# Block 1's opening written out in program order, with w_mod cut into four column stages

## The chip, the cores and the metric

The kernel runs on one core of one Trainium2 chip. The metric is the device time of one execution in microseconds (us). Three timed runs of the kernel before gave 1498.35, 1503.71 and 1503.02 us, a median of 1503.02 us. A profiled execution beside them took 1506.47 us.

Five engines work side by side, each through its own list of instructions: TensorE (PE in the profile, PEld for its weight loads), VectorE (DVE), ScalarE (ACT), GpSimd (POOL) and SyncE (SP). SP and POOL start the DMAs here.

## The reference

Two transformer blocks run one after the other on 256 tokens of 1024 channels. The change touches only the start of the first block and one vector used later in it:

```python
silu_c = jax.nn.silu(c); silu_cc = jax.nn.silu(c_ctx)
mod = silu_c @ w_mod[layer] + b_mod[layer]            # 1024 x 6144
sh1, sc1, g1, sh2, sc2, g2 = jnp.split(mod, N_MOD, axis=-1)
mc = jnp.split(silu_cc @ w_mod[layer] + b_mod[layer], N_MOD)
h  = modulate(rms_norm(x,  norm1_w[layer]), sh1, sc1)     # h*(1+scale)+shift
hc = modulate(rms_norm(xc, norm1_w[layer]), mc[0], mc[1])
q, k, v, g, f = split_proj(h @ wi)
kc = hc @ wi[:, K_OFF:V_OFF]; vc = hc @ wi[:, V_OFF:G_OFF]
```

Shift and scale (sh1, sc1) are needed for both sequences before the first projection. The other four parts of mod are needed for c alone, and later: g1 at the end of the mixer, sh2 and sc2 before the FFN, g2 at its end.

## The kernel before

Activations lie transposed, channels on the 128 partitions: a 1024x256 tensor is eight tiles of 128x256 (KT = 8). For full precision every float32 operand is split into a high float32r part (a cast on ACT, line 245) and a low rest (a subtraction on DVE, line 246), and a product is three float32r matmuls. `weights` loads 512 KB of a weight matrix (two k-tiles of 512 columns) into one of four buffers `wf`, by SP, and splits it into one of three pairs `wh`, `wl`. `lin_units` is a generator: each step loads one such piece and issues its matmuls, with the weights stationary (`mm_b`, result transposed, `psb`) or the activations stationary (`mm_a`, result `psa`). A 512-column projection takes four units.

The opening computes shift and scale for both sequences. `mod_first(j)` takes 512 columns of w_mod in four pieces, multiplies them into `psm` with the two conditioning vectors stationary (lines 446 and 447), copies the 4x512 result to SBUF (`mrow`), turns it into columns with four small transposes (`pst`) and adds the bias. Column groups 0 and 1 are the shift, 2 and 3 the scale. Groups 0 and 2 serve the first four k-tiles, 1 and 3 the last four. `normed` then makes the normalized, scaled and shifted tile of each k (`nt` on DVE, `hxh` on ACT, `hxl` on DVE). The string START (line 30) says in which order these steps, the units of the projections q (w_in piece 0, transposed) and f (piece 6), the load of the context and its sums of squares are issued. From this order a scheduler derives the order on each engine.

After the opening comes the projection `win[1]` (k, for both sequences), then `win[2]` and `win[3]` (v), then the eight retention heads, the gates and so on. Beside their units, `mod_rest` computes the other four parts of mod: it loads w_mod in 512 KB pieces through the same four `wf` buffers, accumulates 128x512 products on DVE into `macc` (lines 476 and 478), and sums over the partitions with four matmuls against a column of ones for each 512 columns (line 482), eight times.

The second block and its experts follow. Their instructions stand in the same order in both kernels.

Of the kernel before, what the change touches and what calls it, by code (L numbers as in the profile page):

```python
# [26 lines left out]
NUP = 11  # L27
TOPK = 16
PH = 8
START = "ssssmqmmmnnnnqffhssssxqlfcqfqf"  # L30
GATES = 8
HEADS = (27, 28, 30, 32)
RING = 8
# [115 lines left out]
def _chunks(w, width=512):  # L149

    k, n = w.shape
    return np.ascontiguousarray(w.reshape(k // P, P, n // width, width).transpose(2, 1, 0, 3))


def _layout(i):

    i = {k: np.asarray(v) for k, v in i.items()}
# [9 lines left out]
    a = {  # L167
        "xt": ft(i["x"][0]), "ct": ft(i["ctx"][0]),
        "vec1": v1, "con1": k1, "cv2": v2, "io": io, "dft": _DFT,
        "lora": np.ascontiguousarray(np.concatenate(  # L170
            [np.concatenate([i["rw_w_up_2"][0], i["rw_a_up_2"][0]], axis=0), i["rw_g_up_2"][0]], axis=1)),
        "wmod": _chunks(i["w_mod"][0]), "win": _chunks(i["w_in"][0]),
        "wro": _chunks(i["w_ret_out"][0]), "wfo": _chunks(i["w_four_out"][0]),
        "wbg": _chunks(i["w_branch_gate"][0]), "wo": _chunks(i["w_out"][0]),
        "wup": _chunks(wup),
# [44 lines left out]
class _Builder:  # L220
# [196 lines left out]
    def block1(self, xt):  # L417
        nc, tc, a, S = self.nc, self.tc, self.a, self.S
        V = self.V1
# [7 lines left out]
        mod = cp.tile([P, 48], F32, name="mod")  # L427
        modc = cp.tile([P, 16], F32, name="modc")

        def mod_load(j, k0):  # L430
            wf = self.wp.tile([P, 1024], F32, tag="wf", name="wf", bufs=4).rearrange("p (k n) -> p k n", k=2)
            nc.sync.dma_start(wf, a["wmod"][j][:, k0:k0 + 2])
            return wf

        cs2 = cp.tile([P, KT, 4], F32R, name="cs2")
        self.split(cs, cs2[:, :, :2], cs2[:, :, 2:])

        def mod_first(j):

            ps = self.ps("psm")  # L440
            for k0 in range(0, KT, 2):
                wh, wl = self.weights(a["wmod"][j][:, k0:k0 + 2])
                for k in range(2):

                    s, e = k0 + k == 0, k0 + k == KT - 1
                    nc.tensor.matmul(ps[:4], cs2[:, k0 + k], wh[:, k], start=s, stop=e, skip_group_check=True)
                    nc.tensor.matmul(ps[:2], cs2[:, k0 + k, :2], wl[:, k], start=False, stop=e, skip_group_check=True)
                if k0 + 2 < KT:
                    yield
# [5 lines left out]
            js = slice(4 * j, 4 * j + 4)  # L455
            t = self.tmp([P, 4, 2], "mt")
            nc.vector.tensor_add(t, pt[:, :4, :2], V("bmod")[:, js, None].to_broadcast([P, 4, 2]))
            nc.vector.tensor_add(mod[:, js], t[:, :, 0], pt[:, :4, 2])
            nc.vector.tensor_add(modc[:, js], t[:, :, 1], pt[:, :4, 3])
            yield  # L460

        def mod_rest():

            accs = [S([P, 512], "macc%d" % i) for i in range(2)]
            wf = mod_load(4, 0)
            for j in range(4, 12):
                acc = accs[j % 2]
                for k0 in range(0, KT, 2):
                    w = wf
                    if k0 + 2 < KT:  # L470
                        wf = mod_load(j, k0 + 2)
                    elif j < 11:
                        wf = mod_load(j + 1, 0)
                    for k in range(2):
                        if k0 + k == 0:
                            nc.vector.tensor_scalar(acc, w[:, k], cs[:, 0, 0:1], None, op0=ALU.mult)
                        else:
                            nc.vector.scalar_tensor_tensor(acc, w[:, k], cs[:, k0 + k, 0:1], acc, op0=ALU.mult, op1=ALU.add)  # L478
                    yield
                pt = self.ps("pst")  # L480
                for n in range(4):
                    nc.tensor.matmul(pt[:, n:n + 1], acc[:, n * P:(n + 1) * P], ones[:, 0:1], start=True, stop=True)
                nc.vector.tensor_add(mod[:, 4 * j:4 * j + 4], pt[:, :4], V("bmod")[:, 4 * j:4 * j + 4])
            S.free("macc0", "macc1")
            yield

        rest = mod_rest()

        m1 = cp.tile([P, 2, KT], F32, name="m1")

        def scales(j):
            js = slice(4 * j, 4 * j + 4)
            for i, m in enumerate((mod, modc)):
                nc.vector.scalar_tensor_tensor(m1[:, i, js], m[:, 8 + 4 * j:12 + 4 * j], 1.0, V("n1w")[:, js], op0=ALU.add, op1=ALU.mult)
        first = mod_first(0)
        next(first)
# [18 lines left out]
        nc.scalar.activation(self.warm, f2[:, :1], AF.Sqrt)
        pulls(first, 3)()
        nc.sync.dma_start(xt, a["xt"])
        r = self.rstd(xt)
        first = mod_first(2)
        pulls(first, 4)()  # L520
        scales(0)
        hc = tuple(S([P, KT, T], "hc" + i, F32R) for i in "hl")
# [8 lines left out]
        def fcopy(ps, b):  # L531
            nc.scalar.copy(f[:, b], ps)
        gq = self.lin_units(a["win"][0], KT, 512, bs=[(hx, self.rope(qt, 0.125))])
        gf = self.lin_units(a["win"][6], KT, 512, as_=[(hx, fcopy)])
        second = mod_first(1), mod_first(3)
        work = {"s": soon, "m": second[0], "n": second[1], "q": gq, "f": gf}
        for i in START:
            if i == "x":
                nc.sync.dma_start(xct, a["ct"])
            elif i == "c":  # L540
                self.busy = True
                rc = self.rstd(xct)
                self.busy = False
            elif i == "h":
                scales(1)
            elif i == "l":
                self.C1 = C = self.blob(a["con1"], self.v1c[1], "con1", "blob", self.wid)
            else:
                next(work[i], None)
# [1070 lines left out]
```

## Time and profile before

| what | value |
|---|---|
| profiled execution | 1506.47 us |
| its span | 1504.7 us |
| median of the timed runs | 1503.02 us |
| PE busy in the span | 1352.3 us (90%) |
| DVE busy | 1048.2 us (70%) |
| ACT busy | 739.0 us (49%) |
| granted TensorE clock, mean | 0.975 |
| HBM read | 410.66 MB |

Busy shares are a mean over stages that have different limits. For this change the first 75 us, and then the stretch up to about 310 us in which mod_rest runs, are what is to be read. "PEclk" is the granted clock as a share of the full 2.4 GHz: 0.50 is the lower level of 1.2 GHz. A matmul's listed duration reaches past the start of the next one; what it costs in a row of matmuls is the distance between their starts.

### The profile page before, as it was taken

What the parts mean: (1) busy time and instruction counts of PE and PEld (TensorE: products, weight loads), DVE (VectorE), ACT (ScalarE), POOL (GpSimd) and SP (SyncE); (2) the same over time, 40 slices, a digit from 0 to 9 for tenths busy, and PEclk for the clock granted to TensorE, in tenths of its full rate; (3) what the DMA queues carried; (4) which work ended last, traced back from release to release, by engine and by line L of the source; (5) the groups of instructions that cost most, each with busy time, mean ns of one, the idle gap of its engine ahead of it and who ended that gap; (6) DMA issues with size and microseconds to landing.
All of it is one profiled execution on the core that took longest, in us unless ns stands there. A gap on an engine that the chain in (4) does not pass through costs nothing.

```text
span 1504.7 us, 21103 instructions
## 1 busy us (share of the span) xinstructions
PE 1352.3 (90%) x7496; PEld 975.6 (65%) x7496; DVE 1048.2 (70%) x2095; ACT 739.0 (49%) x1566; POOL 301.3 (20%) x283
## 2 busy tenths in 40 slices
PE   6999999989999999999999789878978898778786
PEld 3788898989999988899889435323533353223222
DVE  6784876867766778656478777778676775767544
ACT  7533554455555676534465355344434353434433
POOL 0000000000000000000000345443444344434341
PEclk9999999999999999999999899999999999999999
DMA  8655575745555453312147699999999999999995
GB/s 289 226 169 181 176 249 192 245 139 183 183 185 187 147 164 118 113 57 90 52 162 251 269 422 420 422 421 421 409 422 420 421 416 420 421 421 421 421 421 237
DMA packets 76569, 413.07 MB, mean 275 GB/s; under 512 B 8641, under 2 KB 8769, under 8 KB 43313
## 3 DMA queue, kind: packets, MB, share of 16 engines
q0 software_dynamic: 38880, 276.59, 44.5%
q1 hardware_dynamic: 37440, 134.88, 27.6%
q8 instruction: 59, 0.97, 0.3%
q14 instruction: 46, 0.37, 0.1%
q10 hardware_dynamic: 144, 0.26, 0.0%
HBM read 410.66 MB, written 1.05 MB: 274 GB/s over the span
## 4 chain that ended last, share of the span: by engine, by line
PE 51%; DMA 19%; DVE 11%; issue 9%; POOL 5%; ACT 4%; POOLq 0%; SPq 0%; DVEq 0%; ACTq 0%
DMA uv<-in_uv_dram,rows 17%; PE psb L267 9%; PE psb L268 9%; PE psb L269 9%; POOL uv L1487 5%; DVE uv L1494 4%; PE acc L1500 3%; DMA wf<-in_wmod_dram 2%; PE psa L277 2%; PE psa L279 2%; PE psa L278 2%; PE acc L267 1%; PE acc L269 1%; PE acc L268 1%; PE psr L1042 1%
## 5 line engine op out<-in xcount | busy, mean ns | idle before, releaser
L1500 PE MATMUL acc<-uv,dg 128*128 128x512 f32 x1024 | 501.9, 630 | 116.8 <-ACT dg L1498 114.2
L1500 PEld LDWEIGHTS acc<-uv,dg 128*128 128x128 f32 x1024 | 188.1, 196 | 419.7 <-ACT dg L1498 251.3
L1494 DVE CUSTOM_DVE_ANT_0 uv<-uv,hn 128x1024 f32<-128x1024 f32 x256 | 310.2, 1222 | 171.7 <-DMA uv<-in_uv_dram,rows 165.7
L1487 POOL DMA_INDIRECT uv<-in_uv_dram,rows x256 | 283.1, 1106 | 395.1 <-PE acc L1500 268.7
L246 DVE TENSOR_TENSOR wl<-wf,wh 128x1024 fp32r<-128x1024 f32 x213 | 258.2, 1217 | 125.8 <-ACT wh L245 122.6
L245 ACT CAST wh<-wf 128x1024 fp32r<-128x1024 f32 x213 | 221.9, 1044 | 237.3 <-PE psb L268 137.4
L267 PE MATMUL psb<-hxh,wh 128*128 128x256 f32 x960 | 280.3, 292 | 4.7 <-ACT hxh L370 3.4
L268 PE MATMUL psb<-hxl,wh 128*128 128x256 f32 x960 | 274.9, 287 | 0.0
L269 PE MATMUL psb<-hxh,wl 128*128 128x256 f32 x960 | 274.1, 286 | 0.2 <-DVE wl L246 0.2
L1495 ACT ACTIVATE act<-act 128x1 f32<-128x1 f32 x256 | 51.8, 202 | 341.4 <-DVE act L1494 341.3
L267 PEld LDWEIGHTS psb<-hxh,wh 128*128 128x128 f32 x960 | 185.4, 193 | 11.2 <-issue 4.7
L268 PEld LDWEIGHTS psb<-hxl,wh 128*128 128x128 f32 x960 | 185.3, 193 | 3.8 <-issue 2.9
L269 PEld LDWEIGHTS psb<-hxh,wl 128*128 128x128 f32 x960 | 185.2, 193 | 1.1 <-issue 0.3
L1498 ACT ACTIVATE dg<-io,act 128x128 f32<-128x128 f32 x256 | 102.8, 402 | 8.4
L1496 ACT ACTIVATE act<-act,gate 128x1 f32<-128x1 f32 x256 | 75.3, 294 | 8.3
L980 POOL MEMSET mt<- 128x2048 f32 x2 | 3.6, 1816 | 351.9 <-PE psb L269 351.9
L478 DVE SCALAR_TENSOR_TENSOR macc<-wf,cs,macc 128x512 f32<-128x512 f32 x56 | 42.0, 750 | 23.0 <-DMA wf<-in_wmod_dram 22.2
L843 POOL DMA_DIRECT2D wq<-in_wq_dram x12 | 6.3, 529 | 258.1 <-PE pstm L992 138.7
L267 PE MATMUL acc<-fh,wh 128*128 128x256 f32 x176 | 49.5, 281 | 0.0
L268 PE MATMUL acc<-fl,wh 128*128 128x256 f32 x176 | 49.4, 281 | 0.0
L269 PE MATMUL acc<-fh,wl 128*128 128x256 f32 x176 | 49.4, 281 | 0.0
L277 PE MATMUL psa<-wh,hxh 128*128 128x512 f32 x96 | 38.7, 404 | 0.0
(468 smaller groups left out, 2076.9 us busy)
## 6 DMA issues: line engine op xcount, KB each, us to landing
wf<-in_wmod_dram SPq DMA_DIRECT2D x48, 512.0 KB, 4.3
wf<-in_wup_dram SPq DMA_DIRECT2D x44, 512.0 KB, 3.6
wf<-in_win_dram SPq DMA_DIRECT2D x28, 512.0 KB, 4.5
wf<-in_wdn_dram SPq DMA_DIRECT2D x22, 512.0 KB, 3.7
wf<-in_wbg_dram SPq DMA_DIRECT2D x16, 512.0 KB, 4.6
wf<-in_wo_dram SPq DMA_DIRECT2D x16, 512.0 KB, 4.7
wf<-in_wml_dram SPq DMA_DIRECT2D x16, 512.0 KB, 3.7
wf<-in_wg_dram SPq DMA_DIRECT2D x16, 512.0 KB, 3.7
```

Of the source, the lines that this page charges most:

```text
L245: self.nc.scalar.copy(h, src)
L246: self.nc.vector.tensor_sub(l, src, h.bitcast(F32))
L267: nc.tensor.matmul(ps, p, xh[:, k0 + k, :], start=s, stop=False, skip_group_check=True)
L268: nc.tensor.matmul(ps, p, xl[:, k0 + k, :], start=False, stop=False, skip_group_check=True)
L269: nc.tensor.matmul(ps, q, xh[:, k0 + k, :], start=False, stop=e, skip_group_check=True)
L277: nc.tensor.matmul(ps, x, wh[:, k, :n], start=s, stop=False)
L1487: nc.gpsimd.indirect_dma_start(t, None, a["uv"], bass.IndirectOffsetOnAxis(ap=self.rows[b][:, h, k:k + 1], axis=0))
L1494: nc.vector.tensor_tensor_reduce(t[:, :D], t[:, :D], hn[:, b], 1.0, 0.0, ALU.mult, ALU.add, act)
L1495: nc.scalar.activation(act, act, AF.Gelu)
L1496: nc.scalar.activation(act, act, AF.Copy, scale=self.gate[b][:, h, k:k + 1])
L1498: nc.scalar.activation(dg, ident, AF.Copy, scale=act)
L1500: nc.tensor.matmul(acc[b][c], dg, t[:, D + c * 512:D + (c + 1) * 512], start=False, stop=h == PH - 1 and k == TOPK - 1, skip_group_check=True)
```

## The change

The table START goes. The opening is written out in four stages inside `manual_schedule`, under which PE, DVE and ACT keep the order of the program. Stage s computes shift and scale of two k-tiles: w_mod's first 2048 columns come in eight pieces of 256 columns and 1 MB (`wm`), a shift piece and a scale piece per stage, loaded by GpSimd's queue into slots of their own, four ahead. Then follow the split of the two projection pieces of these k-tiles (`ahead`), the columns, two tiles of `normed` and one unit each of q and f. In stage 0, c is also spread over all partitions as `cr` (eight matmuls `pscr`, two copies on ACT).

mod_rest takes w_mod's other columns transposed: each of 32 tiles is 128 outputs by 1024 inputs (`wr`), loaded by SP into slots of its own three ahead, and one multiply-and-sum along the row on DVE gives one column of mod. The matmuls of line 482 go.

```diff
-START = "ssssmqmmmnnnnqffhssssxqlfcqfqf"
...
-        "wmod": _chunks(i["w_mod"][0]), "win": _chunks(i["w_in"][0]),
+        "wmod": _chunks(i["w_mod"][0][:, :2 * D], 256),
+        "wmt": np.ascontiguousarray(i["w_mod"][0][:, 2 * D:].T).reshape(32, P, D), "win": _chunks(i["w_in"][0]),
...
+        def load(i):
+
+            if i < 8:
+                raw[i] = t = S([P, KT, 256], "wm%d" % i)
+                nc.gpsimd.dma_start(t, a["wmod"][i // 2 + 4 * (i % 2)])
+
+        def shift(s, between):
 
             ps = self.ps("psm")
...
+            for i in (2 * s, 2 * s + 1):
+                cols = slice(256 * (i % 2), 256 * (i % 2) + 256)
+                for j in range(2):
+                    w = raw[i][:, 4 * j:4 * j + 4]
+                    wh, wl = (S([P, 4, 256], "w%s%d" % (x, j), F32R) for x in "hl")
+                    self.split(w, wh, wl)
+                    for k in range(4):
+
+                        n = 4 * j + k
+                        nc.tensor.matmul(ps[:4, cols], cs2[:, n], wh[:, k], start=i % 2 == 0 and n == 0, stop=False, skip_group_check=True)
+                        nc.tensor.matmul(ps[:2, cols], cs2[:, n, :2], wl[:, k], start=False, stop=n == 7, skip_group_check=True)
+                    S.free("wh%d" % j, "wl%d" % j)
+                S.free("wm%d" % i)
+                load(i + 4)
+                if i % 2 == 0:
+                    between()
+            return ps
...
+            for n in range(16, 19):
+                load(n)
+            for n in range(16, 48):
+                load(n + 3)
+                nc.vector.tensor_tensor_reduce(w[n], w[n], cr, 1.0, 0.0, ALU.mult, ALU.add, mod[:, n:n + 1])
+                S.free("wr%d" % n)
...
+        with tc.manual_schedule(engines={nc.tensor.engine, nc.vector.engine, nc.scalar.engine}):
+            for s in range(4):
+                ps = shift(s, (lambda: None) if s else sums)
+                ahead(s)
+                if s == 0:
+                    nc.scalar.activation(r, self.pss[:, :T], AF.Sqrt, bias=self.eps, scale=1.0 / D)
+                if s == 0:
+                    nc.vector.reciprocal(r, r)
+                columns(s, ps)
+                for _ in range(2):
+                    next(soon)
+                next(gq)
+                next(gf)
+                if s == 0:
+
+                    cr = S([P, D], "cr")
+                    for i in range(2):
+                        ps = self.ps("pscr")
+                        for k in range(4):
+                            nc.tensor.matmul(ps[:, k * P:(k + 1) * P], cs[:, 4 * i + k, 0:1].to_broadcast([P, P]), ident, start=True, stop=True)
+                        nc.scalar.copy(cr[:, i * 512:(i + 1) * 512], ps)
+                if s == 2:
+                    nc.sync.dma_start(xct, a["ct"])
+                    self.C1 = C = self.blob(a["con1"], self.v1c[1], "con1", "blob", self.wid)
```

ACT before, from the columns of group 0 to those of group 2 (`sq` are the squares of x, `wh` the casts of weights):

```order
L245 CAST wh<-wf 128x1024
L451 COPY mrow<-psm 4x512
L317 ACTIVATE sq<-xt 128x256
L245 CAST wh<-wf 128x1024 x2
L337 ACT_TABLE_LOAD
L337 ACTIVATE rstd<-pss,eps 128x256
L245 CAST wh<-wf 128x1024 x4
L451 COPY mrow<-psm 4x512
```

ACT in the change, from the end of the squares of x in stage 0 to the first casts of stage 1:

```order
L245 CAST wh0_189<-wm1_109 128x1024
L245 CAST wh1_201<-wm1_109 128x1024
L245 CAST wh_216<-wf_215 128x1024
L245 CAST wh_222<-wf_221 128x1024
L542 ACTIVATE rstd_132<-pss_164,eps_67 128x256
L465 COPY mrow_229<-psm_137 4x512
L370 ACTIVATE hxh_133<-nt_242,mod_99 128x256
L370 ACTIVATE hxh_133<-nt_246,mod_99 128x256
L557 COPY cr_290<-pscr_291 128x512
L557 COPY cr_290<-pscr_297 128x512
L245 CAST wh0_304<-wm2_111 128x1024
```

The two copies of `cr` now stand between the tiles of stage 0 and the casts of stage 1. The matmuls `pscr` that they read stand on PE behind the whole first unit of q and of f.

SP before, at the end of the opening (line 432 loads mod_rest's pieces):

```order
L257 DMA wf<-in_win_dram 128x1024 x8
L432 DMA wf<-in_wmod_dram 128x1024 x2
L257 DMA wf<-in_win_dram 128x1024
L432 DMA wf<-in_wmod_dram 128x1024
L257 DMA wf<-in_win_dram 128x1024
```

SP in the change, at the same place (line 485 loads mod_rest's tiles):

```order
L257 DMA wf<-in_win_dram 128x1024 x9
L485 DMA wr_961<-in_wmt_dram 128x1024
L485 DMA wr_963<-in_wmt_dram 128x1024
L485 DMA wr_965<-in_wmt_dram 128x1024
L485 DMA wr_967<-in_wmt_dram 128x1024
L485 DMA wr_1000<-in_wmt_dram 128x1024
L257 DMA wf<-in_win_dram 128x1024
L485 DMA wr_1033<-in_wmt_dram 128x1024
L257 DMA wf<-in_win_dram 128x1024
L485 DMA wr_1066<-in_wmt_dram 128x1024
```

Where one piece of mod_rest stood between two projection pieces, up to five stand now. 25 of the 32 tiles are loaded before the heads begin.

DVE in the change, while `win[2]` and `win[3]` run (ISA is the multiply-and-sum and its read-out):

```order
L246 TENSOR_TENSOR wl<-wf,wh 128x1024
L490 ISA wr_1767,mod<-wr_1767,cr 128x1024
L490 ISA mod 128x1
L490 ISA wr_1836,mod<-wr_1836,cr 128x1024
L490 ISA wr_1899,mod<-wr_1899,cr 128x1024
L490 ISA wr_1968,mod<-wr_1968,cr 128x1024
L246 TENSOR_TENSOR wl<-wf,wh 128x1024
```

Four such sums, each followed by its read-out, now stand between two splits; before, it was two to four products of line 478.

## Rows read from the trace of the kernel before

**Rows 1.** Busy time, PEclk, DMA share and GB/s by stretch of 20 us

```profile
0.00:20.00 20.00, 11.28 (x35) 4.81 (x36) 9.53 (x27) 16.33 (x28) 2.09 (x6) 1.00 0.80 286
20.00:40.00 20.00, 14.20 (x70) 7.21 (x69) 16.58 (x25) 13.37 (x17) 0.00 (x0) 0.83 0.84 288
40.00:60.00 20.00, 18.22 (x97) 14.13 (x96) 13.69 (x25) 12.26 (x20) 0.00 (x0) 0.91 0.84 290
60.00:80.00 20.00, 20.00 (x120) 17.90 (x119) 16.70 (x25) 9.77 (x18) 2.36 (x2) 1.00 0.40 126
...
120.00:140.00 20.00, 20.00 (x88) 16.31 (x88) 10.45 (x13) 5.02 (x6) 0.65 (x1) 1.00 0.62 202
```

**Rows 2.** Timeline (start, duration, idle before in brackets): x, PE's steps and the context's

```profile
13.79 1.95 ACT L317 ACTIVATE sq<-xt 128x256 f32<-128x256 f32 x6 [0.95 <-DMA xt<-in_xt_dram]
...
30.23 0.16 DVE L457 TENSOR_TENSOR mt<-pst,vec 128x8 f32<-128x8 f32 x1
...
30.81 1.28 DVE L365 SCALAR_TENSOR_TENSOR nt<-xt,m,rstd 128x256 f32<-128x256 f32 x3
...
55.84 0.28 PE L267 MATMUL psb<-hxh,wh 128*128 128x256 f32 x1
...
58.72 0.40 PE L277 MATMUL psa<-wh,hxh 128*128 128x512 f32 x1
...
61.47 3.62 PE L325 MATMUL pss<-sq,io 128*128 128x256 f32 x16
...
70.55 1.03 PE L408 MATMUL psr<-rs,con 128*128 128x256 f32 x4
71.22 0.47 PE L267 MATMUL psb<-hxh,wh 128*128 128x256 f32 x1
```

**Rows 3.** The same view as rows 1, by stretches of 2 us

```profile
2.00:4.00 2.00, 0.00 (x0) 0.00 (x0) 0.18 (x2) 0.95 (x3) 0.67 (x1) 1.00 0.89 267
...
12.00:14.00 2.00, 1.39 (x4) 0.24 (x4) 2.00 (x2) 1.05 (x2) 0.00 (x0) 1.00 1.01 416
...
26.00:28.00 2.00, 0.00 (x0) 0.00 (x0) 0.91 (x1) 0.00 (x0) 0.00 (x0) 0.73 0.78 287
28.00:30.00 2.00, 0.42 (x4) 0.42 (x4) 0.91 (x1) 1.52 (x2) 0.00 (x0) 0.50 0.94 377
30.00:32.00 2.00, 2.00 (x7) 0.66 (x7) 1.97 (x9) 0.67 (x2) 0.00 (x0) 0.50 1.03 420
...
48.00:50.00 2.00, 2.00 (x12) 2.00 (x11) 2.00 (x4) 0.37 (x1) 0.00 (x0) 0.50 0.97 364
```

**Rows 4.** Groups of instructions, 0 to 74 us: count, busy us, mean ns, idle before

```profile
L246 DVE TENSOR_TENSOR wl<-wf,wh 128x1024 fp32r<-128x1024 f32 x27 | 32.4, 1219 | 17.0 <-ACT wh L245 17.0
L245 ACT CAST wh<-wf 128x1024 fp32r<-128x1024 f32 x27 | 27.8, 1043 | 15.4 <-PE psb L268 5.5 <-DMA wf<-in_wmod_dram 3.0 <-PE psm L447 2.9
L338 DVE RECIPROCAL rstd<-rstd 128x256 f32<-128x256 f32 x2 | 3.5, 1753 | 1.7 <-ACT rstd L337 1.7
L451 ACT COPY mrow<-psm 4x512 f32<-4x512 f32 x4 | 2.3, 570 | 0.0
L515 ACT ACT_TABLE_LOAD x1 | 1.3, 1283 | 0.0
```

**Rows 5.** Chain of work that ended last: column sums, and 128-column float32 matmuls

```profile
119.26 0.79 PE pst L482 x8
...
155.09 0.45 PE pso L622 x4
```

**Rows 6.** Who waited for whom on PE, 72 to 520 us: total, times, longest

```profile
PE psz L665 <- DVE fs L660: 1.6, 1, 1.6
PE psz L665 <- ACT fs L659: 1.2, 1, 1.2
```

**Rows 7.** Instructions of lines 482 and 1494 (min/median/max ns), groups of line 478

```profile
L482 PE MATMUL pst<-io,macc x64: 164/250/271, 119.1 to 306.2; 128*128 128x1 f32 x64
...
L1494 DVE CUSTOM_DVE_ANT_0 uv<-uv,hn x256: 1204/1224/1290, 845.5 to 1494.2; 128x1024 f32<-128x1024 f32 x128
L1494 DVE DVE_READ_ACCUMULATOR2_ANT act<- x256: 76/83/85, 846.6 to 1495.4; 128x1 f32 x128
...
L478 DVE SCALAR_TENSOR_TENSOR macc<-wf,cs,macc 128x512 f32<-128x512 f32 x56 | 42.0, 750 | 23.0 <-DMA wf<-in_wmod_dram 22.2
```

**Rows 8.** DMA issues of the whole span: queue, KB each, median us to landing

```profile
wq<-in_wq_dram POOLq DMA_DIRECT2D x12, 512.0 KB, 7.4
```

More of the change, by code (lines that the diff above doesn't have):

```diff
@@ L428, in block1, with columns @@
         modc = cp.tile([P, 16], F32, name="modc")
[L430 to L433, printed above, removed]
+        m1 = cp.tile([P, 2, KT], F32, name="m1")
         cs2 = cp.tile([P, KT, 4], F32R, name="cs2")
         self.split(cs, cs2[:, :, :2], cs2[:, :, 2:])
-        def mod_first(j):
-            ps = self.ps("psm")
[L441 to L449, printed above, removed]
+        raw = {}
+        def load(i):
[3 more added lines that the diff above has]
+        def shift(s, between):
+            ps = self.ps("psm")
+            for i in (2 * s, 2 * s + 1):
[14 more added lines that the diff above has]
+            return ps
+        def columns(s, ps):
             row = self.tmp([4, 512], "mrow")
@@ L454, in mod_first @@
                 nc.tensor.transpose(pt[:, n, :], row[:, n * P:(n + 1) * P], ident[:4, :4])
[L455 to L460, printed above, removed]
-        def mod_rest():
[L464 to L484, printed above, removed]
@@ new lines, in columns @@
+            pt = pt[:, :4].rearrange("p (a n) c -> p a n c", a=2)
+            js = slice(2 * s, 2 * s + 2)
+            two = lambda x: x.rearrange("p (a n) -> p a n", a=2)[:, :, js]
+            t = self.tmp([P, 2, 2, 2], "mt")
+            nc.vector.tensor_add(t, pt[:, :, :, :2], two(V("bmod")[:, :16])[:, :, :, None].to_broadcast([P, 2, 2, 2]))
+            for i, m in enumerate((mod[:, :16], modc)):
+                nc.vector.tensor_add(two(m), t[:, :, :, i], pt[:, :, :, 2 + i])
+                nc.vector.scalar_tensor_tensor(m1[:, i, js], two(m)[:, 1], 1.0, V("n1w")[:, js], op0=ALU.add, op1=ALU.mult)
@@ new lines, in mod_rest, with load @@
+        def mod_rest():
+            w = {}
+            def load(n):
+                if n < 48:
+                    w[n] = S([P, D], "wr%d" % n)
+                    nc.sync.dma_start(w[n], a["wmt"][n - 16])
+            for n in range(16, 19):
[4 more added lines that the diff above has]
+                S.free("wr%d" % n)
+                if n % 8 == 7:
+                    js = slice(n - 7, n + 1)
+                    nc.vector.tensor_add(mod[:, js], mod[:, js], V("bmod")[:, js])
+                yield
+            S.free("cr")
@@ L485, in mod_rest @@
             yield
         rest = mod_rest()
[L489 to L496, printed above, removed]
         self.consts()
+        nc.sync.dma_start(xt, a["xt"])
+        for i in range(4):
+            load(i)
@@ L514, in block1, with fcopy, ahead, sums @@
         nc.vector.tensor_mul(f2, V("fnw"), V("fnw"))
[L515 to L522, printed above, removed]
-        hx, soon = self.normed(xt, r, m1[:, 0], mod[:, 0:8])
+        nc.scalar.activation(self.warm, wctx[:, 0, 0, :1], AF.Sqrt)
+        r = self.tmp([P, T], "rstd")
+        hx, soon = self.normed(xt, r, m1[:, 0], mod[:, 0:8])
+        def fcopy(ps, b):
+            nc.scalar.copy(f[:, b], ps)
+        gq = self.lin_units(a["win"][0], KT, 512, bs=[(hx, lambda ps, n0: self.rope(qt, 0.125)(ps, n0))])
+        gf = self.lin_units(a["win"][6], KT, 512, as_=[(hx, fcopy)])
+        def ahead(s):
+            for j in (0, 6):
+                self.ahead.append(self.weights(a["win"][j][:, 2 * s:2 * s + 2]))
+        def sums():
+            self.r1 = self.squares(xt)
+            for _ in self.r1:
+                pass
+        qt = f = None
+        with tc.manual_schedule(engines={nc.tensor.engine, nc.vector.engine, nc.scalar.engine}):
[21 more added lines that the diff above has]
+                    self.C1 = C = self.blob(a["con1"], self.v1c[1], "con1", "blob", self.wid)
         qt = S([P, 4, T], "qt")
@@ L529, in block1 @@
         nc.gpsimd.memset(qz[1][:64], 0.0)
[L531 to L549, printed above, removed]
+        self.busy = True
+        rc = self.rstd(xct)
+        self.busy = False
+        for g in (gq, gf):
+            for _ in g:
+                pass
+        hc = tuple(S([P, KT, T], "hc" + i, F32R) for i in "hl")
         late = self.norming(xct, rc, m1[:, 1], modc[:, 0:8], *hc)
```

## The prediction

> **What bounds the kernel now.** I read the stretches of 20 us first. From 60 us on PE is busy all the time at the full clock, DVE and ACT are not, and this goes on through the projections [rows 1]. What is lost there is lost before 60 us: PE is busy 11.28, 14.20 and 18.22 us of three times 20, and the granted clock is 0.83 and 0.91 in the second and third [rows 1]. The timeline then gives the step at which the opening ends: the first matmul of `win[1]` starts at 71.22 us [rows 2]. So a saving in the opening is worth its full length, one on DVE or in a DMA behind it is worth nothing unless PE waited for it, and one on PE is worth its full length again. In the opening itself no engine is full. DVE's splits waited 17.0 us for ACT's casts, and these for PE's release of buffers 5.5 us and for w_mod 3.0 us [rows 4]: a chain that goes from engine to engine, not a slow load.
>
> **The opening, step by step.** The new order is fixed on PE, DVE and ACT, so I follow it by hand, with durations from the rows.
>
> Loads. GpSimd's queue is not seen beside SP's in this opening. SP's loads alone brought 267 GB/s at 2 to 4 us and 416 at 12 to 14 [rows 3]; I take 340 GB/s from 2 us on, shared evenly. The first 1 MB of w_mod, with as much on SP, is there after 2.1 MB, at 8.5 us; x, which stands behind 0.41 MB on SP, after 2.9 MB at 10.6 (before: ACT got it at 13.79 [rows 2]); the second piece after 4.2 MB, at 14. The bounds: without sharing, 6 us for the first piece and 7 for x; with GpSimd's queue held back, 17 us for the second, since the one load shape from that queue that I have took 7.4 us for 512 KB [rows 8]. I take the middle.
>
> The Trainium skill, "DMA: Bandwidth & Descriptors", section "Queues, rings and completion order", says that each DMA engine takes packets in turn from the queues that have work; "Issuing engines are not separate DMA queues" on the same page adds that issuing from several engines saves only the issue time. By that the change buys no bandwidth, and even sharing is the value to take; by the unshared bound the opening would be 2.5 us shorter. No run here shows the two queues together in the opening.
>
> Stage 0. ACT casts half of piece one (1.04 us), does 0.23 us of decay factors, casts the other half, loads a table (1.28) and is at 12.3. Eight squares of x at 0.325 (1.95 for six [rows 2]) end at 14.9, the first cast of piece two at 15.95. DVE then has four splits at 1.22 [rows 4] to 20.8 and the reciprocal (1.75) to 22.55. Five small operations take 0.6 (30.23 to 30.81 [rows 2]), `nt` and `hxh` 0.5 each. The first unit starts at 24.2 us. Bounds: 21.7 with the early loads, 26.2 with the late ones.
>
> Stage 0 to 1. A unit of q is 24 matmuls at 0.12 us (55.84 to 58.72), one of f 12 at 0.23 (58.72 to 61.47) [rows 2]: 5.6 us. Behind them PE makes `cr`: eight matmuls of 128 columns, two records each, 0.11 us a record (four in 0.45 [rows 5]), 1.8 us. ACT has the two copies of `cr` in its list ahead of stage 1's casts. So ACT stands idle until PE is through, and its next cast starts 5.6 + 1.8 + 0.57 = 8.0 us after the unit began, though the buffers and the weights have been ready for long. From there: one cast, four splits (4.8), the last eight matmuls of `psm` (0.95), `mrow` (0.57 [rows 4]), four transposes (0.4), 0.6, 0.5 and 0.5: 9.4 us. Together 17.4.
>
> ACT's rows show it waiting for PE with work undone [rows 4], but not what stood behind. The Trainium skill, "TensorE: Matmul & The Clock Gate", section "Architectural detail: the array is 16× 32×32, not 1× 128×128", has ACT and DVE as strict first-in-first-out. By that rule the 8.0 us stand; without it stage 1 would cost as much as the next two.
>
> Stages 1 to 2 and 2 to 3. ACT and DVE need 11.3 us: a cast, six splits (7.3), 0.6, and two tiles that go from DVE to ACT and back. PE's loop is longer: unit 5.6, then 32 `psm` matmuls of 256 columns at 0.12, then `mrow`, transposes, columns, `nt` and `hxh` with PE idle: 12.0 us. Twice, 24.0.
>
> End. The last unit (5.6), the context's sums of squares (3.4 of the 3.62 listed [rows 2]) and the first rotation of q (0.7, 70.55 to 71.22 [rows 2]): 9.7. At the full clock `win[1]` starts at 24.2 + 17.4 + 24.0 + 9.7 = 75.3 us.
>
> Clock. After PE stood still from 26 us the granted clock fell to 0.50 (1.2 GHz) and stayed there while PE was busy again, and once more at 48 us [rows 3]. One such stretch full of work costs (1 - 0.91) x 20 = 1.8 us [rows 1]. The new order has a gap of 4 us before stage 0's unit and one of 2.5 us before each of the others. I count two of four, 3.6 us; the bounds are none and four, 7.2.
>
> So `win[1]` starts at 78.9 us, 7.7 later than before. Bounds: 73.0 (early loads, no slow stretch), +1.8; 84.7 (late loads, four stretches), +13.5.
>
> **The rest of mod.** Removed on PE: 32 matmuls of line 482, 64 records [rows 7], 0.79 us for eight [rows 5], all in stretches where PE is full: 6.3 us less. On DVE 56 products of 0.75 us and eight shorter ones go, 32 sums come. One is 1.22 us and its read-out 0.08, as line 1494 has it [rows 7]: 42 us against 46. That is worth nothing by itself. The product waits for w_mod, 22.2 us in all [rows 7], reached PE in one place I can see, at the Fourier step, where PE waited 1.6 and 1.2 us for its copies [rows 6]. There hardly a sum is left; I count half, 1.4 us.
>
> Moved: 25 of 32 sums, and their 512 KB loads, now stand before the heads. From the end of `win[1]` to the last split of `win[3]` DVE has 17 sums (22 us), five splits (6) and 3 us of other work, 31 us, while PE has seven units of 5.6 us, 39. The loads there are 13 MB: 330 GB/s over 39 us, where the row at 120 us shows 202 and rows in the opening 416 [rows 1, 3]. So the cover is 8 us. I charge 1 us; between 0 and 12 (the rival below).
>
> **Sum.** +7.7 - 6.3 - 1.4 + 1.0 = +1.0 us on a profiled 1506.47, so 1507.5 in such an execution. That execution lies 3.45 above the median of the timed runs, hence 1504 us for the median.
>
> **Rivals.**
> 1. Early loads and a clock that holds. The opening then ends at 73.0: +1.8 - 6.3 - 2.8, 1496 us. For it: the peak of 416 GB/s [rows 3], and gaps short enough that part of them may not count. Against it: the 4 us gap in stage 0 is as long as the one that lowered the clock at 26 us.
> 2. The sums hold up the splits (slower). DVE takes its list in order, so a split behind a sum waits for that sum's row. If each of the 17 waits as long as line 478 did (22.2 us in 18 waits, 1.2 us), that is 20 us against a cover of 8: 12 us late on PE, 1503 + 7.7 - 6.3 - 1.4 + 12 = 1515 us. It decides from 0.5 us a sum. For it: five row loads stand in a bunch between two w_in pieces on SP. Against it: the rows are loaded three ahead into slots of their own, where line 478's shared the four buffers of the splits.
> 3. The copies of `cr` hold nothing up, as if ACT could pass them: stage 1 costs 12.0 instead of 17.4, 1499 us.
> 4. Late loads and a slow stretch in each stage: +13.5 in place of +7.7, 1510 us.
>
> **Chances.** The forecast 0.55, rival 1 0.17, rival 2 0.18, rival 3 0.03, rival 4 0.07. The range goes from rival 1's 1496 to 1517, which is rival 2 with part of rival 4. 0.5% is 7.5 us, about what a measurement of this kernel can tell from no change. Faster by more than that (under 1495.5) needs rival 1 and a little more, or rival 3 with early loads: 0.14. Slower (over 1510.5) is most of rival 2, half of rival 4 and the upper edge of the forecast: 0.26. Within: 0.60. The forecast's own range is 1498 to 1511.
>
> **What would show it.** Right: the first unit of q starts near 24 us; ACT waits about 7 us for `pscr` before the first cast of stage 1; units of q start 17, then 12 to 14 us apart; `win[1]` starts at 76 to 82 us; PE is full from there to the heads; no gap at the Fourier step. Wrong: `win[1]` before 73 us (loads, or ACT not held), or PE idle in `win[2]` and `win[3]` with splits behind sums that wait for `wr`.

## The result, and the profile after

The changed kernel takes 1524.12 us (median of four runs, 1522.64 to 1525.89) against 1502.74 us for the kernel before (four runs, 1498.35 to 1503.71). The ratio is 1.0142 with a 95% interval of 1.0128 to 1.0156: slower by 1.4%. The forecast was 1504 us, the range ended at 1517. Its profiled execution took 1524.38 us, with a span of 1522.6 us, 17.9 us more than before.

The stretches of 20 us of the change (columns as in [rows 1]) already show where:

```profile
0.00:20.00 20.00, 8.01 (x33) 5.74 (x33) 5.54 (x20) 11.78 (x24) 3.06 (x9) 1.00 0.93 363
20.00:40.00 20.00, 13.16 (x75) 10.42 (x73) 8.66 (x16) 6.98 (x11) 0.53 (x1) 0.83 0.68 285
40.00:60.00 20.00, 16.31 (x103) 11.76 (x103) 15.01 (x21) 11.12 (x14) 1.35 (x3) 0.91 0.56 205
60.00:80.00 20.00, 15.04 (x81) 11.96 (x82) 12.60 (x24) 10.36 (x16) 1.60 (x2) 0.81 0.37 126
80.00:100.00 20.00, 19.18 (x104) 16.39 (x103) 17.45 (x27) 8.72 (x17) 2.35 (x2) 0.93 0.74 273
```

Before, PE was full from 60 us on [rows 1]. Now it is 15.04 us busy between 60 and 80 at a clock of 0.81, and no other engine is full either. The loads are early (363 GB/s in the first 20 us against 286 in [rows 1]) and then come and go (8 GB/s at 64 to 66 us, in a fence below). Behind stage 0 the opening waits neither for bytes nor for a full engine; it is a chain.

The timeline of PE gives the steps: the first matmul of the four units of q, the second tile's first matmul in the first of them, what follows each pair of units (`pscr`, then `psm` twice, then `pss`), and the first matmul of `win[1]` (71.22 us in [rows 2]). Six of the context's sixteen `pss` matmuls stand inside the fourth pair:

```profile
26.82 0.58 PE L267 MATMUL psb<-hxh,wh 128*128 128x256 f32 x1 [3.51 <-ACT hxh L370]
...
28.28 0.58 PE L267 MATMUL psb<-hxh,wh 128*128 128x256 f32 x1
...
35.26 1.95 PE L556 MATMUL pscr<-io,cs 128*128 128x128 f32 x16
...
47.44 0.38 PE L267 MATMUL psb<-hxh,wh 128*128 128x256 f32 x1 [1.91 <-ACT hxh L370]
...
55.81 0.28 PE L453 MATMUL psm<-wh,cs 128*4 128x256 f32 x1
...
62.57 0.58 PE L267 MATMUL psb<-hxh,wh 128*128 128x256 f32 x1 [1.85 <-ACT hxh L370]
...
71.82 0.28 PE L453 MATMUL psm<-wh,cs 128*4 128x256 f32 x1
...
78.58 0.39 PE L267 MATMUL psb<-hxh,wh 128*128 128x256 f32 x1 [1.85 <-ACT hxh L370]
...
79.48 1.91 PE L325 MATMUL pss<-sq,io 128*128 128x256 f32 x4
...
81.41 1.06 PE L325 MATMUL pss<-sq,io 128*128 128x256 f32 x2
...
87.63 2.32 PE L325 MATMUL pss<-sq,io 128*128 128x256 f32 x10
...
90.46 0.47 PE L267 MATMUL psb<-hxh,wh 128*128 128x256 f32 x1
```

`win[1]` starts 19.2 us later than before. From there to the end of the span it is 1432.1 us against 1433.5: the rest gained only 1.3. The clock in windows of 2 us, in each unit and at the start of the second and fourth, is the surprise (PEclk is the third number from the end):

```profile
26.00:28.00 2.00, 1.18 (x3) 0.79 (x3) 1.10 (x3) 0.80 (x2) 0.00 (x0) 0.50 1.00 421
...
46.00:48.00 2.00, 0.43 (x2) 0.23 (x2) 1.37 (x6) 0.51 (x1) 0.00 (x0) 1.00 1.03 426
...
50.00:52.00 2.00, 2.00 (x11) 2.00 (x11) 2.00 (x2) 2.00 (x3) 0.00 (x0) 0.50 0.47 190
...
64.00:66.00 2.00, 1.97 (x7) 1.74 (x8) 1.54 (x2) 2.00 (x3) 0.00 (x0) 0.50 0.04 8
...
78.00:80.00 2.00, 1.29 (x5) 1.00 (x6) 0.88 (x2) 1.66 (x5) 0.00 (x0) 0.84 0.97 373
80.00:82.00 2.00, 2.00 (x8) 1.64 (x6) 0.62 (x2) 1.78 (x6) 0.00 (x0) 0.50 1.02 383
```

Each of the four units runs for a part at the lower level, 1.2 GHz (0.50). The first and third start there; the second and fourth start at 1.00 and fall about 1 us in. Ahead of the last three PE had stood still only 0.67 us (for `mrow`) and 1.9 us (for the tile), with the four transposes between.

ACT in stage 0 waits for `cr` as forecast, and only then casts for stage 1:

```profile
36.35 0.59 ACT L557 COPY cr<-pscr 128x512 f32<-128x512 f32 x1 [8.13 <-PE pscr L556]
37.24 0.59 ACT L557 COPY cr<-pscr 128x512 f32<-128x512 f32 x1 [0.31 <-PE pscr L556]
37.73 3.90 ACT L245 CAST wh<-wm 128x1024 fp32r<-128x1024 f32 x4
```

And behind the heads, where the forecast had nothing, DVE waits for the small constants of block 2 and then, in a row sum, for its row; the split that PE needs stands behind them:

```profile
203.37 0.17 DVE L810 TENSOR_TENSOR fn<-vec,cv 128x8 f32<-128x8 f32 x1 [3.86 <-DMA cv<-in_cv_dram]
207.30 1.23 DVE L490 CUSTOM_DVE_ANT_0 wr<-wr,cr 128x1024 f32<-128x1024 f32 x1 [3.06 <-DMA wr<-in_wmt_dram]
209.79 1.22 DVE L246 TENSOR_TENSOR wl<-wf,wh 128x1024 fp32r<-128x1024 f32 x1
```

```profile
211.07 0.50 PE L278 MATMUL psa<-wl,hxh 128*128 128x512 f32 x1 [3.52 <-DVE wl L246]
```

The 20 us rows of this stretch show the clock after that wait (0.91), and how little the DMA engines had moved in the heads (77 GB/s) before everything came at once (249):

```profile
160.00:180.00 20.00, 19.99 (x165) 17.51 (x164) 13.06 (x37) 9.97 (x19) 0.83 (x1) 1.00 0.25 77
...
200.00:220.00 20.00, 16.48 (x85) 13.91 (x84) 13.52 (x36) 9.27 (x11) 0.00 (x0) 0.91 0.71 249
```

### The profile page after: what moved, and what is told of

The parts are those of the page before. It is cut to its first block, busy times and chain, and to the rows that moved or that the text cites. A ratio compares the mean times of both kernels' runs of the same rounds, so it can differ in the third digit from the quotient of the medians.

```text
span 1522.6 us, 21072 instructions
## 1 busy us (share of the span) xinstructions
PE 1343.3 (88%) x7512; PEld 976.6 (64%) x7512; DVE 1043.3 (69%) x2095; ACT 737.7 (48%) x1564; POOL 308.2 (20%) x291
## 4 chain that ended last, share of the span: by engine, by line
PE 48%; DMA 23%; DVE 14%; issue 8%; POOL 4%; ACT 3%; POOLq 0%; DVEq 0%; ACTq 0%; SPq 0%
DMA uv<-in_uv_dram,rows 21%; PE psb L267 9%; PE psb L268 9%; PE psb L269 9%; DVE uv L1518 4%; POOL uv L1511 4%; PE psa L278 2%; PE psa L279 2%; PE psa L277 2%; DVE wl L246 1%; PE acc L267 1%; PE acc L268 1%; PE acc L269 1%; PE psr L1066 1%; PE psq L1061 1%
## 5 line engine op out<-in xcount | busy, mean ns | idle before, releaser
L1524 PE MATMUL acc<-uv,dg 128*128 128x512 f32 x1024 | 491.0, 617 | 128.4 <-ACT dg L1522 124.9
L1524 PEld LDWEIGHTS acc<-uv,dg 128*128 128x128 f32 x1024 | 183.4, 192 | 425.0 <-ACT dg L1522 263.0
L246 DVE TENSOR_TENSOR wl<-wf,wh 128x1024 fp32r<-128x1024 f32 x197 | 239.3, 1219 | 139.5 <-ACT wh L245 137.8
L245 ACT CAST wh<-wf 128x1024 fp32r<-128x1024 f32 x197 | 205.7, 1047 | 212.2 <-PE psb L268 129.7
L267 PE MATMUL psb<-hxh,wh 128*128 128x256 f32 x960 | 284.0, 296 | 13.3 <-ACT hxh L370 13.0
L268 PE MATMUL psb<-hxl,wh 128*128 128x256 f32 x960 | 278.8, 291 | 0.3
L490 DVE CUSTOM_DVE_ANT_0 wr<-wr,cr 128x1024 f32<-128x1024 f32 x32 | 38.3, 1221 | 6.4 <-DMA wr<-in_wmt_dram 6.3
L278 PE MATMUL psa<-wl,hxh 128*128 128x512 f32 x96 | 38.7, 403 | 3.5 <-DVE wl L246 3.5
```

Source lines behind the costliest of these rows:

```text
L245: self.nc.scalar.copy(h, src)
L246: self.nc.vector.tensor_sub(l, src, h.bitcast(F32))
L267: nc.tensor.matmul(ps, p, xh[:, k0 + k, :], start=s, stop=False, skip_group_check=True)
L268: nc.tensor.matmul(ps, p, xl[:, k0 + k, :], start=False, stop=False, skip_group_check=True)
L278: nc.tensor.matmul(ps, x, wl[:, k, :n], start=False, stop=False)
L1524: nc.tensor.matmul(acc[b][c], dg, t[:, D + c * 512:D + (c + 1) * 512], start=False, stop=h == PH - 1 and k == TOPK - 1, skip_group_check=True)
```

## The experiments

Two numbers sort them all: when `win[1]` starts (the opening), and how long it is from there to the end of the span (the rest). Of the rest, the part up to the first matmul into `acc` holds all of mod_rest.

| kernel | `win[1]` starts, us | from there to `acc`, us | from there to the end, us | median, us | ratio to before (95%) |
|---|---|---|---|---|---|
| before | 71.22 | 284.5 | 1433.5 | 1502.74 | |
| change | 90.46 | 282.9 | 1432.1 | 1524.12 | 1.0128 to 1.0156 |
| e1 `cr` late | 88.77 | 279.2 | 1429.0 | 1520.73 | 1.0095 to 1.0146 |
| e2 `wm` by SP | 97.29 | 283.3 | 1431.4 | 1529.57 | 1.0139 to 1.0194 |
| e3 old rest | 87.19 | 284.4 | 1431.8 | 1520.44 | 1.0088 to 1.0150 |
| e4 sums only | 70.18 | 281.3 | 1428.3 | 1499.94 | 0.9963 to 0.9990 |
| e5 overlap | 73.75 | 282.6 | 1433.0 | 1506.98 | 1.0016 to 1.0040 |
| e6 tile outer, all | 90.71 | 280.2 | 1438.8 | 1530.45 | 1.0163 to 1.0200 |
| e7 filler | 85.05 | 281.0 | 1431.1 | 1518.58 | 1.0062 to 1.0129 |
| e8 five ahead | 68.47 | 279.2 | 1426.1 | 1498.88 | 0.9956 to 0.9989 |
| e10 all together | 71.73 | 279.5 | 1429.0 | 1500.67 | 0.9969 to 0.9988 |
| e11 tile outer, q | 89.64 | 280.8 | 1431.6 | 1522.78 | 1.0112 to 1.0142 |
| e12 serial | 81.44 | 280.0 | 1428.9 | 1511.10 | 1.0037 to 1.0066 |

The three columns of parts come from one profiled execution of each kernel, and they scatter. Before, e4 and e8 have the same order in their opening and end it at 71.22, 70.18 and 68.47 us. From `acc` on, where the instructions stand in the same order everywhere but in e6, the kernels take 1147.0 to 1150.7 us. So the rest is best read up to `acc`; its first matmul, in the kernel before and in e3 and e8:

```profile
355.74 0.28 PE L267 MATMUL acc<-fh,wh 128*128 128x256 f32 x1
...
371.59 0.28 PE L267 MATMUL acc<-fh,wh 128*128 128x256 f32 x1
...
347.67 0.28 PE L268 MATMUL acc<-fh,wh 128*128 128x256 f32 x1
```

**e1, the copies of `cr` behind stage 3.**

```diff
-                if s == 0:
+                if s == 3:
 
                     cr = S([P, D], "cr")
```

> The eight matmuls and two copies that make cr stand behind stage 3 instead of stage 0; nothing else changes. Theory S (the stages follow one another through ACT, and the copies of cr hold ACT back by about 8 us in stage 0): the first units of q of stages 0 and 1 start 13 to 15 us apart instead of 20.6, ACT no longer waits 8.1 us for pscr, win[1] starts at 83 to 85 us instead of 90.5, time 1516 to 1519 us. Rival L (stage 1 is held by the loads of w_mod, and the copies of cr only stand in time that is lost anyway): distance and time as in the change, 1522 to 1526 us.

1520.73 us. The hold is real: the casts of stage 1 start at 26.93 instead of 37.73 us. But the second unit comes only 4.5 us sooner after the first (16.1 us), the third 1.5 us later after the second, and in the end the eight matmuls stand on PE again, 1.8 us. Neither theory had this: with ACT free, stage 1 is bound by the next thing, PE's own loop of a unit and `psm`. These are its first unit, the `psm` behind it and the next unit:

```profile
25.62 0.58 PE L267 MATMUL psb<-hxh,wh 128*128 128x256 f32 x1 [3.51 <-ACT hxh L370]
...
34.98 0.28 PE L453 MATMUL psm<-wh,cs 128*4 128x256 f32 x1
...
39.48 0.41 PE L468 MATMUL pst<-io,mrow 4*128 4x4 f32 x4 [0.67 <-ACT mrow L465]
...
41.73 0.38 PE L267 MATMUL psb<-hxh,wh 128*128 128x256 f32 x1 [1.85 <-ACT hxh L370]
```

9.4 us for a pair of units that the forecast put at 5.6, then 4.5 for `psm` with its read-out, 2.3 for the tile. From the end of the pair to the next unit it is 6.75 us, where the change takes 12.18: the hold is worth 5.4 us, and the pair, 0.9 us longer here, hides a part of it. This gave the revised theory (P): the unit is what was mis-sized.

**e2, w_mod's pieces by SP.**

```diff
-                nc.gpsimd.dma_start(t, a["wmod"][i // 2 + 4 * (i % 2)])
+                nc.sync.dma_start(t, a["wmod"][i // 2 + 4 * (i % 2)])
...
+        load(0)
         nc.sync.dma_start(xt, a["xt"])
-        for i in range(4):
+        for i in range(1, 4):
             load(i)
```

> The pieces of w_mod are loaded by SP's queue, the first of them ahead of x; GpSimd's queue loads nothing in the opening. Theory S: the first piece is there about 3 us earlier and x no earlier, the four stages keep their distances of 20.6, 15 and 16 us, time 1519 to 1526 us. Rival L (GpSimd's queue brings w_mod late or takes the bandwidth from x, and this is what the opening lost): the opening is shorter by 8 us or more, time under 1516 us.

1529.57 us, above both ranges. The first `psm` does start 2.3 us earlier (8.76 us), but the first unit starts at 32.57 and not 26.82: PE waits 9.06 us for the columns of stage 0, and in 20 to 40 us the clock is 0.57. All of stage 0's pieces now stand in one line, with those of stage 1 ahead of the projections'. Rival L is out: without GpSimd's queue the opening is 6.8 us longer. How much of this is the one queue and how much the order in it was not tried apart.

**e3, the opening of the change with the old rest of mod, and e4, the old opening with the row sums.** In e3 the products of lines 476 and 478 and the matmuls of ones come back, without `cr`; in e4 the new `mod_rest` stands behind START's opening, `cr` made after it.

> The opening of the change, without cr, and the rest of mod as in the kernel before (products on DVE through the wf buffers, matmuls of a column of ones). Theory S: the opening is that of e1 (win[1] at 83 to 85 us), and the rest of mod returns to its cost of before, 2 us more than row sums: time 1517 to 1521 us, 1 to 4 us above e1. Rival R (the row sums with their loads are what costs, in the projections and behind the heads): at least 5 us below e1, under 1512 us.

> The opening of the kernel before with START, and the rest of mod as row sums; cr is made behind the opening. Theory S: win[1] starts within 3 us of before (71.2 us), the matmuls of ones are gone, the stall in the gs projection may stay: time 1497 to 1502 us, that is 1 to 6 us below the kernel before. Rival R: 1508 us or more.

1520.44 and 1499.94 us. So the opening alone costs (e3 against before) about 18 us and the row sums alone (e4 against before) gain about 2.5. Rival R is out. Theory S had e3 1 to 4 us above e1, and their medians cannot be told apart; up to `acc` e3 takes 284.4 us, as before, and e1 279.2. e4 still has the late row: PE waits 2.5 us for a split in the gs projection (the gate, behind the heads), where the kernel before waits for none.

**e5, the stages overlapped.** `cr` goes ahead of the loop; casts, splits and `psm` of stage s+1 go between q's and f's unit of stage s.

```diff
             for s in range(4):
-                ps = shift(s, (lambda: None) if s else sums)
-                ahead(s)
...
                 next(gq)
+                if s < 3:
+                    ps = shift(s + 1, lambda: None)
+                    ahead(s + 1)
+                    columns(s + 1, ps)
                 next(gf)
```

> The four stages overlap: cr is made first, ahead of the loop, and the casts, splits and psm matmuls of stage s+1 stand between the unit of q and the unit of f of stage s, on all three engines. Nothing else changes; the same instructions are issued. Theory P (the opening is lost because PE goes through unit, psm and columns of one stage after another, and stands still for 3 us in each until the next tile is there): a stage falls from 16 us to PE's own work of 10.5 us or DVE's of 9.9, the units of q start 11 to 12 us apart, win[1] starts at 67 to 72 us, time 1499 to 1505 us. Rival D (ACT and DVE, or the loads, could not go faster anyway): units stay 14 us or more apart, win[1] at 77 us or later, time 1509 us or more.

1506.98 us, `win[1]` at 73.75 (the line below): the same instructions in another order give back 16.7 of the 19.2 us. The units of q start 13.5, 11.2 and 11.7 us apart. It misses theory P's range by 2 us: the first pair of units still runs at 0.50, and two row sums, for which `cr` is now ready early, stand among stage 3's tiles on DVE. Up to `acc` its rest is only 1.9 us shorter than before, as the late row holds PE up 3.8 us here.

```profile
73.75 0.47 PE L267 MATMUL psb<-hxh,wh 128*128 128x256 f32 x1
```

**e6 and e11, a transposed unit tile by tile.** e6 for every projection, e11 for q's units alone.

```diff
+                for k in range(st):
+                    for i in range(n // P):
+                        self.mm_b(pl[i // 2][:, i % 2], [y[:, k:k + 1] for y in w], x, k0 + k, 1, i * P, s and i % 2 == 0 and k == 0, e and k == st - 1)
```

> The change with one loop turned: a transposed unit does all its column groups with its first k-tile and then all with its second, where each group took both. The same matmuls. Theory P (the 1.46 us that each of the four units waits for its second tile after three matmuls is paid in full): that wait is covered by the nine other matmuls of the first tile, 1.0 to 1.3 us less per stage, time 1517 to 1520 us. Rival W (the tile chain sets the end of the unit, and the wait only moves): 1521 to 1526 us.

> The change with the loop turned for the units of q alone (e6 had turned it for every transposed projection, so that the bias, sigmoid and convolution steps behind them came later too). Theory P: q's unit falls from 5.7 us to 4.9 as in e6, and nothing else is touched: 2 to 4 us less than the change, time 1518 to 1522 us. Rival W (the wait only moves to the next tile chain): 1523 to 1526 us.

e6 lost 6 us, none of it in the opening and none up to `acc`: from there on it takes 1158.6 us, where the change takes 1149.2. It answers a question that was not asked, and what in those later projections costs it was not pursued. e11 does ask it: q's second unit falls from 5.63 to 4.88 us (47.27 to 52.15), the first three distances by 0.70, 0.78 and 0.63, 2.1 in all. Of this 0.8 us reaches `win[1]`, since its first unit began 0.5 us later and its last stage took 0.8 longer. In time it is no difference that these runs can tell. The wait for the second tile is a true but small term, about 0.7 us a stage. The second units of q and f in e11:

```profile
47.27 0.38 PE L267 MATMUL psb<-hxh,wh 128*128 128x256 f32 x1 [1.89 <-ACT hxh L373]
...
52.15 0.40 PE L277 MATMUL psa<-wh,hxh 128*128 128x512 f32 x1
```

**e7, filler matmuls where PE stands still.**

```diff
                 columns(s, ps)
+                fill = self.ps("psfl")
+                for k in range(14 if s else 20):
+                    nc.tensor.matmul(fill[:, :P], ident, ident, start=True, stop=True)
```

> The change with matmuls that compute nothing (14 of identity by identity per stage, 20 in stage 0, into a PSUM tile that nobody reads) on PE between the transposes of the columns and the first unit, where PE stands still for 3 us. Theory P (PE standing still is what the granted clock of 0.50 in each of the four units follows): clock near 1.00 in the units, 1.5 to 2 us less per unit, time 1516 to 1519 us. Rival C (the clock falls in these units whatever PE did before, or the fillers stand in the way): clock 0.50 again, time 1522 to 1528 us.

1518.58 us, theory P. The clock is 1.00 in every one of the stretches shown above, and the pair of units takes 6.0 us:

```profile
50.00:52.00 2.00, 2.00 (x13) 1.75 (x12) 2.00 (x3) 2.00 (x3) 0.00 (x0) 1.00 0.03 12
...
64.00:66.00 2.00, 2.00 (x13) 1.74 (x12) 2.00 (x3) 2.00 (x3) 0.00 (x0) 1.00 0.03 8
```

```profile
44.08 3.39 PE L548 MATMUL psfl<-io 128*128 128x128 f32 x28
47.23 0.36 PE L267 MATMUL psb<-hxh,wh 128*128 128x256 f32 x1
...
50.52 0.40 PE L277 MATMUL psa<-wh,hxh 128*128 128x512 f32 x1
...
53.27 0.28 PE L453 MATMUL psm<-wh,cs 128*4 128x256 f32 x1
```

q's part falls from 5.63 us (47.44 to 53.07 in the change) to 3.29; e11 puts 0.75 of these 2.3 on the tile, so about 1.6 are the clock. Work that computes nothing brought `win[1]` 5.4 us forward and the median down by 5.5 (the intervals of the two ratios just touch), though the filler ends about a microsecond after the tile is ready.

**e8, rows five ahead.**

```diff
-                load(n + 3)
+                load(n + 5)
```

> e4 (opening of before, row sums) with the rows of w_mod loaded five ahead instead of three. Theory Q (at 180 to 190 us PE waits 2.5 us for a split that stands behind a row sum whose row is late, because the rows, cv and w_in come together after the heads, in which the DMA engines are nearly idle): two more rows are there before that stretch, PE's wait and the slow clock behind it go, 2 to 4 us less than e4, 1496 to 1498 us. Rival B (the bytes of that stretch are too many whatever the order): as e4, 1499 to 1501 us.

1498.88 us against e4's 1499.94, whose runs overlap: in time not told apart. In the profile PE's wait for that split falls from 2.5 to 1.6 us, and the clock of 180 to 200 us rises from 0.91 to 1.00. But with three rows ahead e1 and e12 wait 1.65 and 1.54 us at the same place, without a slow clock behind it, and with five e10 waits 1.97. The wait is there in every kernel with row sums, 1.5 to 3.8 us. So theory Q's cure is not borne out: that five rows shorten the wait is not shown.

**e12, the serial order without hold and slow clock.** e7 with `cr` made ahead of the loop.

> The stages one after another as in the change, but with cr made first and with e7's fillers: neither ACT's hold nor the slow clock is left. What remains above the kernel before is the price of the serial order alone. Theory P: stages of 14 us as in e7's second and third, also for the first; units of q at 27.5, 41.5, 55.5, 69.5, win[1] at 79 to 80 us, time 1510 to 1514 us. Rival A (hold and clock were all of it): win[1] at 75 us or earlier, time under 1507 us.

1511.10 us. Units of q at 29.40, 43.68, 57.65 and 71.61, `win[1]` at 81.44. The start is 2.6 us later than in the change (its first w_mod piece came later, the first `psm` at 12.77 us against 11.10, and the filler adds the rest); the distances are 14 us as expected, and about 1 of them is the filler's overhang. So the serial order alone, at full clock, still ends 10.2 us after the kernel before, and rival A is out. The first and last units of q and `win[1]`:

```profile
29.40 0.36 PE L267 MATMUL psb<-hxh,wh 128*128 128x256 f32 x1
...
71.61 0.36 PE L267 MATMUL psb<-hxh,wh 128*128 128x256 f32 x1
...
81.44 0.47 PE L267 MATMUL psb<-hxh,wh 128*128 128x256 f32 x1
```

**e10, all of it together.** e5's order, the second copy of `cr` at the end of stage 3, a filler ahead of the first unit, e11's loop, rows five ahead.

> All that helped, together: e5's overlapped stages; the second copy of cr at the end of stage 3, so that no row sum can stand among the tiles of the opening (in e5 two of them stood in stage 3 and cost 1.9 us); 18 filler matmuls ahead of the first unit; q's units tile by tile; rows five ahead. Theory P: win[1] at 69 to 71 us instead of e5's 73.95, and 2 us less behind the heads, time 1496 to 1501 us, at or below the kernel before. Rival: what is taken from one step comes back in the next (DVE's 10 us of splits per stage set the pace), time 1503 to 1507 us as e5.

1500.67 us. The stages are 11.4, 11.0 and 11.0 us:

```profile
28.57 0.36 PE L267 MATMUL psb<-hxh,wh 128*128 128x256 f32 x1
...
39.98 0.28 PE L267 MATMUL psb<-hxh,wh 128*128 128x256 f32 x1
...
50.99 0.28 PE L267 MATMUL psb<-hxh,wh 128*128 128x256 f32 x1
...
61.98 0.28 PE L267 MATMUL psb<-hxh,wh 128*128 128x256 f32 x1
...
71.73 0.47 PE L267 MATMUL psb<-hxh,wh 128*128 128x256 f32 x1
```

The clock is 1.00 in all of them:

```profile
20.00:40.00 20.00, 18.48 (x136) 14.38 (x135) 17.43 (x28) 11.68 (x17) 1.58 (x3) 1.00 0.98 394
40.00:60.00 20.00, 18.46 (x137) 14.11 (x136) 17.20 (x27) 14.04 (x17) 1.90 (x2) 1.00 0.45 162
```

It beats the kernel before by 0.2% (0.9969 to 0.9988), and so do e4 and e8. But its opening, with all repairs, only reaches what START had: 71.73 against 71.22 us (70.18 and 68.47 in e4 and e8). What is gained is the row sums': 279.5 us up to `acc` against 284.5.

## Why the prediction was wrong

The forecast was +1 us, the measured time +21. The views and the mechanisms were mostly the right ones; the largest miss is one term that was sized from a row that belongs to another situation, and counted four times.

| step | forecast, us | measured, us | difference |
|---|---|---|---|
| first unit of q starts | 24.2 | 26.82 | +2.6 |
| stage 0 to 1 | 17.4 | 20.62 | +3.2 |
| stage 1 to 2 | 12.0 | 15.13 | +3.1 |
| stage 2 to 3 | 12.0 | 16.01 | +4.0 |
| last unit to `win[1]` | 9.7 | 11.88 | +2.2 |
| slow clock, apart | 3.6 | in the stages | -3.6 |
| `win[1]` starts | 78.9 | 90.46 | +11.6 |
| the rest, against before | -6.7 | -1.3 | +5.4 |
| profiled execution to median | -3.45 | -0.26 | +3.2 |

**The step that failed is "A unit of q is 24 matmuls at 0.12 us (55.84 to 58.72), one of f 12 at 0.23 (58.72 to 61.47) [rows 2]: 5.6 us."** These durations come from 56 to 61 us of the kernel before, where the tiles had long been ready and PE ran at the full clock. In the change the pair takes 8.4, 8.4, 9.25 and 9.05 us; the last holds six of the context's sums, so what it lost is read from the last stage, 2.2 us. Over the four stages the pairs cost 11.4 us more than forecast, of which the separate clock term had 3.6: the remaining 7.8 are two thirds of what the opening missed. Two things are in it. The unit starts when its first tile is ready, and the second follows 1.46 us later (26.82 and 28.28), after three matmuls; e11 shows that it costs about 0.7 us a stage. And the clock is 0.50 in a part of all four units. "I count two of four" was the place where the rows gave bounds and the forecast chose the middle; e7 shows the right end was four, at about 1.6 us each and more in the third. The gap of 2.5 us before each unit had been worked out in the prediction; only its consequence was halved. The kernel before had it too, in its two slow stretches [rows 1, 3].

The Trainium skill, "TensorE: Matmul & The Clock Gate", section "HAM oscillation — how this bites in real kernels", describes a loop in which PE waits once in each round and starts every round at the low clock. The trace of the change agrees in part: there is a slow stretch in each of four rounds, but two of the rounds start at 1.00 and fall about 1 us in; with e7's fillers none is left. The page advises to restructure the loop so that PE stays busy, which is what e5 does.

**The hold by `cr` was right, and so was its price.** ACT waited 8.13 us; forecast were about 7 of waiting and 8.0 between the unit's start and the next cast (here 10.9, the longer unit again). Without it stage 1 did not cost the 12 of rival 3: e1 measured 16.1, 4.5 us less than the change. But behind the pair of units e1 gains 5.4 us (12.18 to 6.75), which is the 5.4 that rival 3 took off; its pair is 0.9 us longer, the mis-sized term again. The Trainium skill, "TensorE: Matmul & The Clock Gate", section "Architectural detail: the array is 16× 32×32, not 1× 128×128", has ACT as strictly first-in-first-out; the trace agrees: in e1, where the copies stand elsewhere, stage 1's casts start 10.8 us earlier.

**The first unit** was 2.6 us late. The first w_mod piece came at about 10 us, not 8.5. Then the last two squares of x waited 1.6 us for PE's sums of the earlier ones, a wait that the forecast put at nothing, and the first cast of piece two started at 17.79 us instead of 14.9. The start of `psm` varies from 10.6 to 13.0 us over the kernels with this opening, so this term scatters by about 2 us from kernel to kernel.

**The rest of mod.** The terms of -6.3 and -1.4, 7.7 together, are nearly borne out. Up to `acc` e8 takes 279.2 us against 284.5, 5.3 less, and in it PE still waits 1.6 us for a split behind a late row: without that wait it is 6.9. For the change it is 1.6 gained, and the 5.3 of the next sentence lost. e3, with the old rest behind the same opening, takes 284.4, as before. Of the two waits at the Fourier step [rows 6] one of 1.2 is left in the change; in e3 the second is 0.36, so it varies without the row sums too. Rival 2's mechanism (a split stands behind a sum that waits for its row) was real too, but the forecast looked for it in `win[2]` and `win[3]`, where PE stayed full, and it struck in the gs projection, behind the heads: 3.5 us of wait and (1 - 0.91) x 20 = 1.8 us of slow clock in 200 to 220 us, 5.3 together. `cv`, the projections' pieces and the rows arrive there together, after heads in which the DMA engines move little (77 GB/s). The forecast walked the moved loads through one stretch and not through the next, and charged them 1.0 us.

**The median.** 3.45 us were subtracted because the profiled execution before lay that far above its median. That was a property of that one execution, not of the kernel: the change's lies 0.26 us above its own.

**The rivals.** Rival 1 is out (it needed `win[1]` at 73). Rival 3 is out (ACT waited). Rival 4 had the right clock and nearly the right start (26.2, measured 26.82), and still put `win[1]` at 84.7, 5.8 us too early. None priced a unit with a slow clock and a late tile together, nor the wait behind the heads, and the range ended 7 us too early. (By the forecast's own terms its bounds for `win[1]` are 72.8 and 84.5, not 73.0 and 84.7; nothing hangs on it.)

The question behind it was not asked at all: why START had mixed the stages. Its string puts steps of the second half's shift and scale (`m`, `n`) between the first unit of q and the next, so PE has other work while a tile is made. e12 and e5 give the price of taking that away, to within the 2.7 us by which START's own opening scatters: 10.2 us for serial stages even at full clock, 2.5 us with the stages overlapped again.

## What to carry to other kernels

A duration read from a full stretch is not the duration behind a wait: before a row is used for a step that starts just when its data arrive, ask what the clock is after that wait and whether all of its data have arrived. When an opening written out in stages replaces a mixed one, write down PE's loop for one stage (work, then stillness until the next tile); stillness in each round is paid twice, once as itself and once as slow clock. Put the next stage's independent work into it before anything else, and follow moved loads through every later stretch in which transfers bunch.

## What the runs showed of the hardware

A standstill of 0.67 and 1.9 us with four small transposes between was followed by 0.50 in three units of three, in two of them about 1 us after the unit had begun. In e10 only the 0.67 us was left in each stage, and the clock was 1.00 through all four units. Idle time of PE before a unit therefore cost more than itself: filling it with matmuls without a purpose brought `win[1]` 5.4 us forward.

The two queues together moved 414 to 436 GB/s at 20 to 30 us, against 420 from SP alone in the highest row shown of before [rows 3]: hardly more at the peak, but more of the early time filled.
